# A 32 KB input moved from ScalarE's DMA queue to third place in GpSimd's list of transfers

## The chip, the cores and the metric

One core of a Trainium2 chip. The metric is device microseconds per execution. The state of a run is "fast" unless it lies over 1.5% above the fastest run of its kernel; ratios and comparisons use fast runs alone. A kernel is called faster or slower from 2% on.

In the profiles PE is TensorE, PEld its loads of weights, DVE VectorE, ACT ScalarE, POOL GpSimd and SP SyncE; a name such as ACTq is the part of an engine that issues instructions. q0 is GpSimd's DMA queue, q1 SyncE's and q10 ScalarE's. A packet is a piece of a transfer as the profile lists it; the 4-byte ones at the end of each transfer are called semaphore packets, since the count that a waiting engine looks at (a semaphore) comes with them. A page cuts the span into 40 slices, and a digit is the busy share of a slice in tenths (9 is 90% or more). PEclk is the share of TensorE's full clock that was granted.

## The reference

```python
x: (32, 256) float32, y: (32, 256) float32, weight: (128, 256, 256) float32
out = np.einsum('bi,bj,kij->bk', x, y, weight)        # (32, 128)
```

The weights are 33.55 MB and each is used once for each of the 32 rows of the batch; x and y are 32 KB each.

## The kernel before

The weights come in 32 groups. Two groups (FIRST) are loaded as float32 by SyncE (`w_f`) and cast by ScalarE; thirty are loaded and cast to bfloat16 on the way by GpSimd, in eleven transfers. These grow from 2 MB read to 8 MB and then become ever smaller, so that little work is left after the last. TensorE multiplies them by a block form of x into PSUM, the memory for its sums, used here as eight banks, and VectorE multiplies the sums by y and reduces over j. So y is not needed before the first unit of 16 groups is through TensorE.

```python
sw = [nc.gpsimd.dma_start(out=w_of(groups)[...], in_=rows_of(groups)[...]).then_inc(s, 16).ins
      for (groups, lo, hi), s in zip(LOADS, s_w)]           # eleven transfers
hw = [
    nc.scalar.dma_start(out=x_sb, in_=x).then_inc(s_x, 16).ins,
    nc.scalar.dma_start(out=y_sb, in_=y).then_inc(s_y, 16).ins,
]
for n, g in enumerate(FIRST):
    hw.append(nc.sync.dma_start(out=w_f[:, n:n + 1, :], in_=rows_of((g,))).then_inc(s_f[n], 16).ins)
# ... all of them are put ahead of the barrier that opens the program ...

# VectorE: first x (x_rep, xt, mask, xblk), then y:
t = done(v.transpose(out=yt, in_=y_sb...)._wait_ge(s_y, 16))
t = done(v.tensor_copy(out=y_rep, in_=yt...)._wait_ge(s_dve, t))
# ... four transposes y_rep -> y4 ...

for u, unit in enumerate(UNITS):          # 16, 8, 4, 2, 1, 1 groups
    # ... TensorE waits until the banks are free and each load has landed; matmuls ...
    # VectorE: prod = sums * y4 (frees the banks), acc = reduce(prod)
```

## Time and profile before

| | before |
|---|---|
| time, median of the first 3 runs | 85.0 us (84.89 to 85.02) |
| span of the profiled run | 83.4 us |
| first DMA packet / last weights landed | 1.2 us / 81.06 us |
| PE, DVE, ACT, POOL busy | 32.6, 24.8, 5.3, 8.2 us |
| y: issued / prepared / first used | 0.57 / 13.80 / 57.78 us |

### The profile page before, as it was taken

The page shows a single profiled execution, that of the slowest core. Times are in us where ns is not written, and L with a number is a line of the kernel's source. Part 1 is how long each engine was busy: PE and PEld are TensorE (multiplying, and loading weights), DVE is VectorE, ACT ScalarE, POOL GpSimd, SP SyncE. Part 2 cuts the span into 40 slices and gives each one's busy share as a digit, 9 for nine tenths or more (in the row PEclk, how much of TensorE's full clock was granted, in tenths as well). Part 3 has the DMA queues.
Part 4 walks back from the last instruction along what each step waited for, and adds up shares of the span by engine and source line. Part 5 has one row for each costly group of instructions (what it writes and reads, how often), then busy time and mean ns, then how long its engine had stood idle before and what let it go on. Part 6 is the DMA issues. An engine that isn't in the chain of part 4 may idle for free.

```text
span 83.4 us, 257 instructions
## 1 busy us (share of the span) xinstructions
PE 32.6 (39%) x136; PEld 4.3 (5%) x43; DVE 24.8 (30%) x28; ACT 5.3 (6%) x5; POOL 8.2 (10%) x17
## 2 busy tenths in 40 slices
PE   0000000000000000000099999997009999995780
PEld 0000000000000000000000000000000100112330
DVE  0038595000000000000000000002999900899932
ACT  0039830000000000000000000000000000000000
POOL 5999300000000000000000000000000000000000
PEclk9999999999999999999999999999995699999999
DMA  3999999999999999999999999999999999999980
GB/s 126 383 360 311 216 216 214 210 214 218 214 218 210 214 212 218 218 216 212 212 212 218 216 218 210 214 212 218 216 214 210 218 212 216 218 214 208 203 120 8
DMA packets 4928, 17.91 MB, mean 215 GB/s; under 512 B 384, under 2 KB 832, under 8 KB 4672
## 3 DMA queue, kind: packets, MB, share of 16 engines
q0 software_dynamic: 4400, 15.73, 94.3%
q1 hardware_dynamic: 432, 2.11, 6.7%
q10 hardware_dynamic: 96, 0.07, 0.3%
HBM read 33.62 MB, written 0.02 MB: 404 GB/s over the span
## 4 chain that ended last, share of the span: by engine, by line
DMA 47%; PE 39%; DVE 6%; another core or an unknown queue 2%; POOL 2%; issue 2%; POOLq 0%
DMA w_sb<-in_weight_dram 47%; PE ps L236 39%; DVE tmp L293 5%; POOL w_sb L120 2%; DVE tmp L301 1%; POOL const-float32-0.0 L331 0%; POOLq L331 0%; POOL const-uint8-127 L331 0%; POOL const-float32-1.0 L331 0%; DVE acc L301 0%
## 5 line engine op out<-in xcount | busy, mean ns | idle before, releaser
L236 PE MATMUL ps<-w_sb,xblk 128*128 128x512 bf16 (+1 forms) x136 | 32.6, 398 | 48.7 <-DMA w_sb<-in_weight_dram 43.9
L293 DVE TENSOR_TENSOR tmp<-ps,y 128x4096 f32<-128x4096 f32 (+3 forms) x4 | 8.6, 2153 | 48.4 <-PE ps L236 48.4
L297 DVE TENSOR_REDUCE acc<-tmp 128x16 f32<-128x4096 f32 (+3 forms) x4 | 8.6, 2155 | 0.1
L236 PEld LDWEIGHTS ps<-w_sb,xblk 128*128 128x128 bf16 x43 | 4.3, 101 | 76.9 <-DMA w_sb<-in_weight_dram 42.7
L120 POOL DMA_DIRECT2D w_sb<-in_weight_dram x11 | 7.5, 700 | 0.6 <-issue 0.6
L177 ACT CAST w_sb<-w_f 128x1024 bf16<-128x1024 f32 x4 | 4.0, 1042 | 0.4 <-DMA w_f<-in_weight_dram 0.4
L191 DVE COPY x_rep<-x_sb 32x1024 f32<-32x1024 f32 x1 | 0.7, 724 | 5.6 <-PEq L331 5.6
L226 DVE STREAM_TRANSPOSE y<-y_rep 32x256 f32<-32x256 f32 x4 | 1.7, 435 | 0.1
L197 DVE STREAM_TRANSPOSE xt<-x_rep 32x256 f32<-32x256 f32 x4 | 1.7, 434 | 0.1
L177 ACT ACT_TABLE_LOAD x1 | 1.3, 1283 | 5.5 <-PEq L331 5.5
L209 DVE TENSOR_SCALAR xblk<-xt,mask 128x256 bf16<-128x256 f32 x4 | 1.4, 501 | 0.0
L301 DVE CUSTOM_DVE_ANT_0 tmp<-ps,y 128x256 f32<-128x256 f32 x2 | 0.9, 426 | 1.6 <-PE ps L236 1.4
L221 DVE COPY y_rep<-yt 32x1024 f32<-32x1024 f32 x1 | 0.7, 682 | 0.0
L204 DVE TENSOR_REDUCE mask<-ident 128x4 f32<-128x128 f32 x1 | 0.4, 380 | 1.0 <-POOL ident L168 1.0
L218 DVE STREAM_TRANSPOSE yt<-y_sb 32x256 f32<-32x256 f32 x1 | 0.4, 446 | 0.0
L168 POOL TENSOR_SCALAR_AFFINE_SELECT ident<-ident 128x128 f32<-128x128 f32 x1 | 0.3, 287 | 0.1
L167 POOL MEMSET ident<- 128x128 f32 x1 | 0.3, 289 | 0.0
L301 DVE DVE_READ_ACCUMULATOR2_ANT acc<- 128x1 f32 x2 | 0.2, 84 | 0.0
L331 POOL MEMSET const-float32-0.0<- 128x1 f32 x1 | 0.1, 99 | 0.2 <-issue 0.2
L331 POOL MEMSET const-bfloat16-1.0<- 128x1 bf16 x1 | 0.1, 102 | 0.0
L331 POOL MEMSET const-uint8-127<- 128x1 uint8 x1 | 0.1, 102 | 0.0
L331 POOL MEMSET const-float32-1.0<- 128x1 f32 x1 | 0.1, 99 | 0.0
## 6 DMA issues: line engine op xcount, KB each, us to landing
w_sb<-in_weight_dram POOLq DMA_DIRECT2D x2, 4096.0 KB, 48.5
w_sb<-in_weight_dram POOLq DMA_DIRECT2D x2, 2048.0 KB, 43.6
w_f<-in_weight_dram SPq DMA_DIRECT2D x2, 1024.0 KB, 6.9
w_sb<-in_weight_dram POOLq DMA_DIRECT2D x2, 1024.0 KB, 41.2
w_sb<-in_weight_dram POOLq DMA_DIRECT2D x1, 512.0 KB, 72.6
w_sb<-in_weight_dram POOLq DMA_DIRECT2D x1, 256.0 KB, 73.3
w_sb<-in_weight_dram POOLq DMA_DIRECT2D x1, 128.0 KB, 73.4
w_sb<-in_weight_dram POOLq DMA_DIRECT2D x2, 64.0 KB, 73.1
```

Source lines behind the costliest of these rows:

```text
L120: nc.gpsimd.dma_start(out=w_of(groups)[:, :, lo * J:hi * J], in_=rows_of(groups)[:, :, lo * J:hi * J],).then_inc(s, 16).ins
L177: c = act.copy(out=w_sb[:, place_of[g], lo:hi], in_=w_f[:, n, lo:hi])
L191: t = done(v.tensor_copy(out=x_rep, in_=x_sb.rearrange("b (ip ic) -> b ic ip", ic=IC).unsqueeze(3) .to_broadcast([B, IC, IP, KK]),)._wait_ ...
L197: c = v.transpose(out=xt[q * 32:(q + 1) * 32, :, :], in_=x_rep[:, :, q * IP // Q:(q + 1) * IP // Q, :],)
L204: t = done(v.tensor_reduce(out=mask, in_=ident.rearrange("p (ip kk) -> p kk ip", kk=KK), axis=AX, op=add,)._wait_ge(s_pool, 2))
L209: c = v.tensor_scalar(out=xblk[:, :, :, kk], in0=xt, scalar1=mask[:, kk:kk + 1], scalar2=None, op0=mult,)
L221: t = done(v.tensor_copy(out=y_rep, in_=yt.unsqueeze(3).to_broadcast([B, J // 32, B, KK]),)._wait_ge(s_dve, t))
L226: c = v.transpose(out=y4[q * 32:(q + 1) * 32, :].rearrange("p (jb j) -> p jb j", j=32), in_=y_rep[:, :, q * BQ:(q + 1) * BQ, :],)
L236: return pe.add_instruction(mybir.InstMatmult(name=nc.get_next_instruction_name(), engine=mybir.EngineType.PE, ins=[pe.lower_ap(rhs), pe.l ...
L293: t = done(v.tensor_tensor(out=prod, in0=sums, in1=y4.unsqueeze(1).to_broadcast([P, n_g, J]), op=mult,)._wait_ge(s_pe, n_pe))
L297: done(v.tensor_reduce(out=acc[:, unit[0]:unit[-1] + 1:unit[1] - unit[0]], in_=prod, axis=AX, op=add,)._wait_ge(s_dve, t))
L301: done(v.tensor_tensor_reduce(out=prod[:, 0, :], in0=sums[:, 0, :], in1=y4, scale=1.0, scalar=0.0, op0=mult, op1=add, accum_out=acc[:, uni ...
```

## The change

The intent is to clear the beginning: y no longer stands in a hardware queue beside `w_f`, and ScalarE has one issue less. y is loaded where there is time for it, behind the first two weight transfers.

```diff
+    sw.insert(2, nc.gpsimd.dma_start(out=y_sb, in_=y).then_inc(s_y, 16).ins)
+
     hw = [
         nc.scalar.dma_start(out=x_sb, in_=x).then_inc(s_x, 16).ins,
-        nc.scalar.dma_start(out=y_sb, in_=y).then_inc(s_y, 16).ins,
     ]
```

Nothing else moves on any engine.

## The prediction

> **What bounds the kernel now.** I read the slices of the span first, to see which resource never rests; then the chain that ended last, in order of time, to see where the end is set; then the DMA issues and the timeline of the first microseconds, because the change sits there.
>
> The slices and queues on the page:
>
> ```profile
> span 83.4 us, 257 instructions
> ...
> DMA  3999999999999999999999999999999999999980
> ...
> q0 software_dynamic: 4400, 15.73, 94.3%
> q1 hardware_dynamic: 432, 2.11, 6.7%
> q10 hardware_dynamic: 96, 0.07, 0.3%
> HBM read 33.62 MB, written 0.02 MB: 404 GB/s over the span
> ```
>
> The 16 DMA engines are full in 37 of 40 slices, from about 2 us to about 80 us, while PE works 39% of the span and DVE 30%. Nearly all of it is q0, the weights that GpSimd issues. The file of weights is 33.55 MB (128 x 256 x 256 x 4 bytes), so the time is the time to read it, plus a start and a tail.
>
> The chain of waits, in order of time (start, length, what):
>
> ```profile
> 2.65 39.16 DMA w_sb<-in_weight_dram
> ...
> 41.86 15.90 PE ps L236 x64
> ...
> 57.78 4.44 DVE tmp L293
> ...
> 62.32 8.75 PE ps L236 x32
> 71.07 0.08 another core or an unknown queue
> ...
> 74.81 1.19 another core or an unknown queue
> ...
> 77.93 0.53 another core or an unknown queue
> ...
> 79.53 0.18 another core or an unknown queue
> ...
> 81.10 0.30 PE ps L236
> ...
> 81.42 0.43 DVE tmp L301
> ```
>
> The page counts 47% for DMA and 39% for PE, but the reader should not take PE for a second bound. Each matmul group from 71 us on waits again for a transfer (the steps called "unknown queue"; the timeline names the releaser of 76.04, 78.50 and 79.75 as DMA of the weights). PE, which starts at 41.86 only when the third load has landed, has caught up with the stream by 71.07 and then follows it. What comes after the last landing is short: one matmul of 0.30 us, one DVE pass of 0.43 us and the output transfer. So the end is the instant when the last weight byte lands, near 81.06 us, plus a fixed tail of 2.3 us. A delay in PE's start is forgiven up to 0.08 + 1.19 + 0.53 + 0.18 = about 2.0 us before it moves the end; a delay of the stream is forgiven nowhere.
>
> The first microseconds and the two transfers of the change:
>
> ```profile
> 0.12 0.41 ACTq L128 DMA_DIRECT2D x_sb<-in_x_dram  x1
> ...
> 0.57 0.44 ACTq L129 DMA_DIRECT2D y_sb<-in_y_dram  x1
> 1.06 7.53 POOL L120 DMA_DIRECT2D w_sb<-in_weight_dram  x11 [0.61 <-issue]
> 5.55 1.28 ACT L177 ACT_TABLE_LOAD   x1 [5.55 <-PEq L331]
> 5.59 0.72 DVE L191 COPY x_rep<-x_sb 32x1024 f32<-32x1024 f32 x1 [5.59 <-PEq L331]
> ...
> 10.78 0.45 DVE L218 STREAM_TRANSPOSE yt<-y_sb 32x256 f32<-32x256 f32 x1
> 11.26 0.68 DVE L221 COPY y_rep<-yt 32x1024 f32<-32x1024 f32 x1
> 11.97 1.83 DVE L226 STREAM_TRANSPOSE y<-y_rep 32x256 f32<-32x256 f32 x4
> ```
>
> y is issued at 0.57 us, is prepared by DVE from 10.78 to 13.80 us without any wait, and is first used by the product at 57.78 us: 44 us of slack. The page of issues gives its way to landing:
>
> ```profile
> x_sb<-in_x_dram ACTq DMA_DIRECT2D x1, 32.0 KB, 1.7
> y_sb<-in_y_dram ACTq DMA_DIRECT2D x1, 32.0 KB, 4.5
> ```
>
> x and y are equally large, but y needs 4.5 us: its packets wait behind the first megabyte of w_f on the same engines. That wait also costs nothing today.
>
> **What the Trainium skill says.** "DMA: Bandwidth & Descriptors", section "Issuing engines are not separate DMA queues": transfers run on the same 16 DMA engines whichever engine issues them, and issuing from several saves only sequencer time. The trace agrees as far as it can: between 5.7 and 8.4 us q0 and q1 each have about half of the engines and the total stays where it was. So moving y should move its work, not remove it. Same page, "Queues, rings and completion order": each DMA engine takes turns between queue rows packet by packet. In this trace the turn is coarse: y, issued at 0.57, is served between 3.6 and 4.7 us, after most of the first w_f. Same page, "Why a DMA increments its semaphore by 16 and not by 1": a transfer from GpSimd posts on all 16 engines, and 32 rows split evenly over 16. The trace shows that shape for y already: 32 packets of 1 KB and 16 of 4 bytes. Same page, "Specifications", has a first byte after about 1 us for GpSimd's path and 0.6 us for ScalarE's; with tens of microseconds of slack the 0.4 us does not matter, and in this trace q0's first packet comes at 5.6 us, with w_f ahead of it.
>
> **The change part by part.**
>
> Removed from ScalarE: one issue of 0.44 us. ScalarE then sits until 5.55 us in the opening barrier, released by others. Worth on the path: 0.
>
> Removed from the early stream: y's packets. Between 3 and 5 us they took 1.69 us of engine time in all (32 packets of about 46 ns, 16 of 9 ns), over 16 engines 0.106 us. The engines were full from 1.4 us on, so w_f and everything behind it come about 0.1 us earlier.
>
> Added to GpSimd: one issue, third of 12. The eleven have a mean of 700 ns, the small ones 548 to 616 ns, so I take 0.57 us. The nine later loads are issued that much later, the last at 8.57 in place of 8.00 us. The first two loads (6 MB read) keep q0 occupied until about 22 us (their landings are at 12.6 and 22.3 us); the third load's issue slips from 2.65 to about 3.2 us, so q0 has 19 us of work in hand. Worth: 0.
>
> The opening barrier: GpSimd joins it at 5.35 us, when its sixth issue of eleven has begun; its sequencer runs about five issues ahead. With twelve, it would join about when the seventh begins, at 5.9 us. DVE's and ScalarE's first work then starts 0.5 to 0.6 us later, and the mask and the copies of w_f end near 12 us in place of 11.2. PE does not start before 41.86. Worth: 0.
>
> Added to the stream q0: 32 packets of 1 KB and 16 semaphore packets, between load two and load three. q0's nearest packets, 512 bytes written from 1 KB read, take 60 ns and its semaphore packets 22 ns; per engine 2 x 60 + 22 = 0.142 us. Packets overlap somewhat at the end of the stream (0.25 us there held 101 packets, 40 ns per packet and engine), so it may be nearer 0.10 us. I take 0.12.
>
> DVE: yt now waits for y, which lands just after load two, near 22.4 us. A new idle of about 11 us appears before that transpose, and y's work of 3.0 us ends near 25.5 us in place of 13.8. The first product at 57.78 is still 32 us away. Worth: 0.
>
> Sum for the last landing: -0.106 + 0.12 = about +0.01 us, anywhere from -0.03 to +0.05. PE's start moves by the same amount. The tail is unchanged. Predicted time: 85.0 us, as before.
>
> **The rivals.**
>
> 1. *The small transfer breaks the stream.* If q0 had to drain at y's end, each engine would idle for the time of a round trip; x alone in an empty machine needs 1.7 us from issue to landing, so this could cost up to about 1.5 us (86.5 us, just within 2%). Against it: q0 already passes ten ends of transfers, and around the landing of load two, at 21.9 to 22.3 us, the engines stay as full as before. Even the last four loads, of 32 to 256 packets, follow one another without a hole. Chance about 3%.
>
> 2. *The early part gets faster.* If y's packets hold up w_f and thereby q0's start by more than their own time, removing them would win some tenths: 84.5 to 84.8 us. For it: q0's first packet comes only at 5.6 us, 4.5 us after its issue. Against it: in the meantime q1 keeps all engines busy, so an earlier q0 only changes the order of the same bytes.
>
> 3. *GpSimd becomes the bound at the start.* If 0.57 us more of issuing, or a longer descriptor ring (275 packets an engine in q0 now, 278 after), delayed q0's first packet, DMA would go idle. w_f alone would last until about 6.9 us (2.1 MB at the 380 to 390 GB/s of 2 to 6 us), so q0 may slip by 1.3 us unnoticed; and y stands third, so the first two issues do not move at all. If the ring were full at 276, GpSimd would pause and the late loads would still come many microseconds ahead of need. Time: 85.0 to 85.2 us.
>
> 4. *y arrives too late.* If it were served after all weights it would set the end. The place in the list forbids it: 22 us against a need at 57.8 us.
>
> **Range and chances.** The sum is under 0.1 us, the three runs of before span 0.13 us, and rivals 2 and 3 reach 0.3 to 0.5 us at most. I give 85.0 us, with 84.7 to 85.3 us to hold eight times in ten. The borders of 2% are 83.3 and 86.7 us. No part of the change can give 1.7 us, since the stream keeps its bytes; only an unforeseen break of the stream could cost it. Faster 1%, within 2% 97%, slower 2%.
>
> **What would show it right or wrong.** Right: the DMA row full from the second slice to the 38th; q10 halved to 48 packets and q0 at 4448; the sum of the queues' shares unchanged; DVE's yt waiting for y until about 22.4 us and working until about 25.5; GpSimd's twelve issues near 8.1 us; DVE's first copy near 6.1 us; PE starting within 0.1 us of 41.86; the last landing within 0.1 us of 81.06. Wrong: a slice near 22 us under full (rival 1), a start of PE earlier than 41.6 us (rival 2), a dip in the third or fourth slice (rival 3), or a first product later than 57.8 us by more than PE's own shift (rival 4).

## More of the kernel before

One view is missing there: who waited for whom, longest first (engine, line, what it waited for: us in total, times, longest).

```profile
DVE tmp L293 <- PE ps L236: 48.4, 2, 44.0
PE ps L236 <- DMA w_sb<-in_weight_dram: 43.9, 4, 41.9
...
PE ps L236 <- DVE tmp L293: 4.6, 1, 4.6
```

No line has y in it: nobody waited for it. The large waits are for weights. The last line will matter: TensorE's second unit waits 4.6 us for VectorE's first product, since the first unit fills all eight banks. That is how a late y could do harm.

## The result, and the profile after

| | before | after |
|---|---|---|
| median of 6 runs each | 84.94 us (84.89 to 85.02) | 84.92 us (84.73 to 84.94) |
| ratio, 95% interval | | 0.9991 (0.9978 to 1.0004) |
| last weights landed (one trace each) | 81.06 us | 81.13 us |

A ratio is the mean time of one kernel's fast runs over that of the other's fast runs of the same rounds, so it is not quite the ratio of the medians. It is the same time. The page of the changed kernel, its slices and queues:

```profile
DMA  4999999999999999999999999999999999999980
...
q0 software_dynamic: 4432, 15.76, 94.3%
q1 hardware_dynamic: 432, 2.11, 6.8%
q10 hardware_dynamic: 48, 0.03, 0.1%
```

The DMA row is as full as before, also in the eleventh slice (20.9 to 22.9 us), where y now passes. ScalarE's queue q10 has lost half of its packets; GpSimd's q0 has gained 32.

The chain of the changed kernel (start, length, what):

```profile
2.65 0.52 POOL y_sb L127
3.17 38.71 DMA w_sb<-in_weight_dram
...
41.93 15.77 PE ps L237 x64
...
74.83 1.28 another core or an unknown queue
...
81.17 0.30 PE ps L237
```

y's issue has entered the chain with 0.52 us, and the step behind it has become shorter by 0.45 us: 38.71 in place of 39.16. That is a trap in reading a chain. The third weight transfer was issued later, but it was issued 19 us before its turn, so the wait behind the issue took up the delay and TensorE began at 41.93 in place of 41.86 us.

The timeline, for the parts that moved:

```profile
2.64 0.53 POOL L127 DMA_DIRECT2D y_sb<-in_y_dram  x1
...
6.08 0.79 DVE L192 COPY x_rep<-x_sb 32x1024 f32<-32x1024 f32 x1 [6.08 <-PEq L332]
...
22.48 0.43 DVE L219 STREAM_TRANSPOSE yt<-y_sb 32x256 f32<-32x256 f32 x1 [10.95 <-DMA y_sb<-in_y_dram]
...
23.67 1.83 DVE L227 STREAM_TRANSPOSE y<-y_rep 32x256 f32<-32x256 f32 x4
```

The opening barrier ends 0.5 us later, as GpSimd has one more issue to get through, and VectorE waits 10.95 us for y. Both are new, both are large beside the effect on the time, and neither costs anything. The first product is 32 us away.

### The profile page after: what moved, and what is told of

It is laid out like the page before. It is cut to its first block, busy times and chain, and to the rows that moved or that the text cites. A ratio compares the mean times of both kernels' runs of the same rounds, so it can differ in the third digit from the quotient of the medians.

```text
span 83.4 us, 257 instructions
## 1 busy us (share of the span) xinstructions
PE 32.6 (39%) x136; PEld 4.3 (5%) x43; DVE 25.1 (30%) x28; ACT 5.2 (6%) x5; POOL 8.8 (11%) x18
## 3 DMA queue, kind: packets, MB, share of 16 engines
q0 software_dynamic: 4432, 15.76, 94.3%
## 4 chain that ended last, share of the span: by engine, by line
DMA 46%; PE 39%; DVE 6%; POOL 3%; another core or an unknown queue 3%; issue 2%; POOLq 0%
DMA w_sb<-in_weight_dram 46%; PE ps L237 39%; DVE tmp L294 5%; POOL w_sb L120 2%; POOL y_sb L127 1%; DVE tmp L302 1%; POOL const-float32-0.0 L332 0%; POOLq L332 0%; POOL const-uint8-127 L332 0%; POOL const-float32-1.0 L332 0%; DVE acc L302 0%
## 5 line engine op out<-in xcount | busy, mean ns | idle before, releaser
L127 POOL DMA_DIRECT2D y_sb<-in_y_dram x1 | 0.5, 534 | 0.0
```

What stands on the lines that cost most here:

```text
L127: sw.insert(2, nc.gpsimd.dma_start(out=y_sb, in_=y).then_inc(s_y, 16).ins)
```

## The experiments

The theory under test: the time is set by the stream of transfers, y costs that stream its own packets wherever it stands, and everything else (issue, barrier, y's landing) lies in slack. The rivals: a small transfer breaks the stream; the crowded beginning was the cost; GpSimd's issuing sets the start; the third place matters.

### What one small load costs the stream, on either queue

A change of 0.1 us or less cannot be seen in 85 us, so the load was multiplied. Eight more copies of y go into spare tiles, behind the original, once on each queue. VectorE waits for all.

```diff
+    for n in range(8):    # nine_pool: in the changed kernel
+        sw.insert(3 + n, nc.gpsimd.dma_start(out=y_more[n], in_=y).then_inc(s_ym[n], 16).ins)
```

> The changed kernel with eight more copies of y loaded by GpSimd right behind y (into spare tiles, VectorE waits for all before it prepares y). Theory (the stream of transfers sets the end and a small transfer costs only its own packets, 96 + 22 ns per engine as measured for y): 8 x 0.118 us = 0.94 us more, or 0.89 if packets overlap as the weights' do; time 85.8 us. Rival (each end of a transfer drains the queue, 1 to 1.5 us each): 93 to 97 us. Rival (small transfers hide beside the big ones): 84.9 us.

```diff
+    for n in range(8):    # nine_act: in the kernel before
+        hw.append(nc.scalar.dma_start(out=y_more[n], in_=y).then_inc(s_ym[n], 16).ins)
```

> The kernel before with eight more copies of y loaded by ScalarE right behind y. Theory (same work on the same engines, whoever issues): 8 x 0.106 us = 0.85 us more than before, time 85.8 us, within 0.15 us of the nine loads by GpSimd. Rival (the place matters: at the beginning there is spare room, in the stream there is none): 84.9 to 85.2 us here against 85.8 there.

| | median | ratio to before (95%) |
|---|---|---|
| nine loads by GpSimd | 85.6 us | 1.0086 (1.0071 to 1.0100) |
| nine loads by ScalarE | 85.96 us | 1.0126 (1.0107 to 1.0145) |
| before, same rounds | 84.88 us | |

Both are slower by about what packets cost, and by nothing like the 8 to 12 us of a drained queue. Eight loads more by ScalarE make 0.0126 x 84.88 = 1.07 us, 0.134 us each. Eight more by GpSimd, against a kernel of the same rounds that has one (y_first, below, 0.9992), make 0.0094 x 84.88 = 0.80 us, 0.10 us each (both to about 0.02 us, from the intervals). The expectation that the two runs would lie within 0.15 us of each other failed: they are 0.34 us apart (0.0040 x 84.88), the intervals do not overlap, and the small loads on ScalarE's queue cost more. The queue line of each page says where (queue, kind: packets, MB, share of 16 engines); first the nine loads by ScalarE, then those by GpSimd:

```profile
q10 hardware_dynamic: 480, 0.33, 1.5%
```

```profile
q0 software_dynamic: 4688, 16.02, 94.4%
```

q10 grew from 96 to 480 packets, 48 a load, and from 0.3% to 1.5% of the engines. From the single packets, which the trace keeps behind these rounded shares, the time in q10 went from 0.231 to 1.268 us per engine, 0.130 us a load; in q0 from 78.648 in the changed kernel to 79.523, 0.109 us a load. GpSimd's loads have 32 packets each (4688 - 4432 = 8 x 32). So the packets account for both costs, and a load by GpSimd is cheaper by 0.02 to 0.03 us. On ScalarE's queue the 1 KB packets took 56 ns and the 4-byte ones 17 ns on average, where those of y alone took about 46 and 9 ns. The two runs differ in the queue and in the place (the crowded beginning, the middle of the stream); which of them lengthens the packets was not tested.

### No y at all

```diff
-    sw.insert(2, nc.gpsimd.dma_start(out=y_sb, in_=y).then_inc(s_y, 16).ins)
+    t = done(v.memset(y_sb, 1.0))        # VectorE, ahead of the transpose; the result is wrong on purpose
```

> No load of y at all (y is set to one by VectorE, so the result is wrong on purpose). Theory: the stream is shorter by y's own packets alone, 0.1 us: 84.8 us. That bounds what any other place of y can win. Rival (y's queue or its issue disturbs the start, whoever issues it): 84.0 to 84.5 us.

Measured: 84.69 us, ratio 0.9974 (0.9958 to 0.9991), and a wrong result. So 0.22 us less, with an interval from 0.08 to 0.36 us. The 0.1 us expected is within it, and the 0.4 us at the near edge of the rival's range is just outside. The saving shows in the times alone: in the one trace of each, the last weights landed at 81.09 us without y and at 81.06 before. This is the most that any place of y can win: about a quarter of a per cent.

### y in other places of the list

Each is the changed kernel with another number in `sw.insert`: 0 (first), 3 (fourth), 4 (fifth).

> y as the first of GpSimd's list in place of the third. Theory: the first weights are issued 0.53 us later, but the engines are busy with w_f until then, so 84.9 us, first weight packet between 5.6 and 6.2 us, no hole in the DMA row. Rival (GpSimd's issue sets the start of the stream): 85.4 to 85.5 us.

Measured: 84.79 us, 0.9992 (0.9976 to 1.0008). The first weight is issued 0.68 us later (1.74 in place of 1.06 us), and the first weight packet of q0 comes at 6.2 us in place of 5.6; the packets that q0 has from 5.5 us on are y's. The DMA row still shows 9 in every slice from the second to the 38th, for the engines are busy with `w_f` meanwhile. So what the rival feared does not happen.

> y as fourth in GpSimd's list, behind the third load. It lands near 42 us and is prepared by about 45 us, still 12 us ahead of the first product. Theory (only the deadline of the first product counts): 84.9 us. Rival (the third place is special): more than 85.3 us.

Measured: 84.83 us, 0.9998 (0.9977 to 1.0019). VectorE waits 30.6 us for y and begins with it at 42.1 us; it costs nothing.

> y as fifth, behind the fourth load. It lands near 61.5 us, is prepared at 64.6 us, 6.8 us after the first product could have begun. Theory (PE waits for the bank that this product frees; part of the delay is forgiven): following VectorE's and PE's queue of work from there gives 88.5 to 90.3 us. Rival (the end follows the last weight alone): 85 us.

Measured: 89.97 us, 1.0608 (1.0556 to 1.066), inside the expected range. The chain:

```profile
61.38 0.44 DVE yt L219
...
64.51 4.44 DVE tmp L294
...
69.05 9.39 PE ps L237 x32
...
78.46 2.30 DVE tmp L294
```

y is there only at 61.38 us, the first product begins at 64.51 in place of 57.72 us, and TensorE has the banks for its second unit at 69.05 in place of 62.26 us. So the third place is nothing special: first, third and fourth are one time, and the border lies between the fourth place and the fifth, where y's preparation ends 12 us before and 6.7 us after the first product could begin.

### How much lateness of the first product is forgiven

y_fifth delayed the product by 6.8 us and cost 5 us. To measure alone how much of such a delay is forgiven, an additional product of k groups is put ahead of the first one on VectorE, into a spare tile.

```diff
+        if u == 0:
+            done(v.tensor_tensor(out=spare[:, :k, :], in0=sums[:, :k, :],
+                in1=y4.unsqueeze(1).to_broadcast([P, k, J]), op=mult)._wait_ge(s_pe, n_pe))
         if n_g > 1:
             t = done(v.tensor_tensor(out=prod, in0=sums, ...
```

k = 4:

> The additional product with 4 groups (128x1024, 1.21 us). VectorE's queue after its second product forgives 1.7 us, by the trace of the kernel before; so 84.9 us where PE runs at full clock, up to 85.4 us in runs in which the second group of matmuls falls into the half clock as with 7 groups. If nothing were forgiven: 86.1 us.

k = 7:

> The changed kernel with an additional product of 7 groups (128x1792, about 2.0 us) on VectorE ahead of the first product, so that the banks are freed and PE resumes 2.0 us later. The prediction forgave 2.0 us, counted from PE's waits for transfers: then 84.9 us. If VectorE's own queue is tighter (its products at 75.6, 78.0 and 79.6 us follow one another within 0.1 us, and only 1.4 us are free ahead of the last one): 0.5 us more, 85.4 us.

k = 16:

> The same with all 16 groups, about 4.45 us of delay. Forgiven 2.0 us: 87.3 us. Forgiven 1.4 to 1.5 us: 87.9 us. Nothing forgiven: 89.3 us. All forgiven: 84.9 us.

| k | added | median | ratio to before (95%) |
|---|---|---|---|
| 4 | 1.2 us | 85.1 us | 1.0028 (1.0000 to 1.0056) |
| 7 | 2.0 us | 86.01 us | 1.0115 (1.0074 to 1.0156) |
| 16 | 4.4 us | 87.62 us | 1.0298 (1.0256 to 1.0340) |

With k = 7, forgiveness of 2.0 us would have left the time as it was; it rose by 0.0115 x 84.9 = 0.98 us, more than either case expected (84.9 or 85.4 us). One of the six runs with k = 7, at 86.62 us, counts as slow; it is in the median and not in the ratio. The chain for k = 7 shows what became the bound:

```profile
64.61 9.91 PE ps L238 x32
...
74.54 2.30 DVE tmp L300
...
76.87 2.29 DVE acc L304
79.16 1.14 DVE tmp L300
...
83.20 0.34 DVE tmp L308
```

From 74.54 us on it is VectorE without a pause, to 83.54 us: 9.00 us of its own work. In the kernel before, the same work begins at 71.11 us and could end at 80.11, and it ends at 81.86 because it waits for the last weights; so VectorE's queue forgives 1.75 us. In this trace it began 3.43 us late: 2.02 us for the added product, and most of the rest from TensorE, whose 32 matmuls took 9.91 in place of 8.75 us and whose first unit ended 0.35 us later. 3.43 - 1.75 = 1.68 us, which is the delay of the end (83.54 against 81.86). The clock row of the page explains the slower matmuls; before, then k = 7:

```profile
PEclk9999999999999999999999999999995699999999
```

```profile
PEclk9999999999999999999999999999655559999997
```

The spell of half clock lasts about five slices in place of two. How long it lasts differs from run to run (mean granted clock 0.934 to 0.960 in these fast runs), and their times are spread over 1.2 us, while the kernel before is spread over 0.4 us. k = 16 went the other way. Its chain and clock row:

```profile
66.39 8.37 PE ps L238 x32
...
74.78 2.30 DVE tmp L300
```

```profile
PEclk9999999999999999999999999999955589999999
```

Here the second unit begins when most of the spell is over, and takes 8.37 us. By the clock records of the three traces, 3.41 us of this unit ran at half clock before, 5.76 us with k = 7 and 2.64 us with k = 16; less half of that, its 32 matmuls took 7.04, 7.03 and 7.05 us. So the clock accounts for the whole difference. Over the runs with k = 16 the time rose by 0.0298 x 84.9 = 2.53 us of 4.42 added: 1.9 us were forgiven (1.5 to 2.25 by the interval), against 1.0 us with k = 7 (0.7 to 1.4).

So what is forgiven is not one number. VectorE's queue allows 1.75 us after the second unit (1.88 us, reckoned in the same way from the trace of the changed kernel), and TensorE's second unit adds to it or takes from it, as more or less of it falls into the spell of half clock. A longer spell alone cost nothing: it lasts 6.8 us in the traces without y and with x moved (below), and these runs are no longer than the others. With k = 4, where 84.9 to 85.4 us was expected, the six runs fall into two sets, three at 84.77 to 84.94 and three at 85.26 to 85.39 us; the mean clock does not separate them, and this stays open.

### x as well, and the changed kernel once more

```diff
-        nc.scalar.dma_start(out=x_sb, in_=x).then_inc(s_x, 16).ins,
+    sw.insert(1, nc.gpsimd.dma_start(out=x_sb, in_=x).then_inc(s_x, 16).ins)
```

> x goes to GpSimd's list as well, behind the first weights, so that ScalarE issues nothing. x lands near 12.6 us, and PE's other operand is ready near 17 us, 25 us before PE begins. Theory A (x's packets now run before w_f's first packet, in engines that are otherwise idle, so they are free where they are): 0.1 us slower than the changed kernel, 85.0 us. Theory B (x stands ahead of w_f in the engines and delays it): 0.1 to 0.2 us faster, first w_f packet before 1.3 us in place of 1.4.

Measured: 84.93 us, 1.0003 (0.9983 to 1.0023). The first packet of `w_f` still comes at 1.4 us with nothing ahead of it, so theory B's mechanism is absent. Theory A's cost of 0.1 us is too small to be told from none here: the single traces have the last weights at 81.26 in place of 81.13 us, which agrees with it but is one trace each.

> The changed kernel, unaltered, once more. The runs with nine loads differ by 0.0040 in their ratios, which over nine loads makes 0.04 us per load in favour of GpSimd; so 0.9991 to 1.0000, not to be told from the same. If the change wins more than its own packets: under 0.998.

Measured: 84.92 us, 1.0001 (0.9980 to 1.0023), as expected. No version was found that beats both kernels.

## Why the prediction was right

The time was predicted as 85.0 us and is 84.92. By its steps:

- **The bound.** Right. Eight more small loads in either place lengthen the run by about the time of their packets, while a barrier 0.5 us later, a wait of 11 or even 30 us on VectorE and an issue 0.5 us later leave it as it is.
- **The issue by GpSimd.** Taken as 0.57 us, measured 0.53; the barrier moved DVE's first copy to 6.08 us (predicted near 6.1). Placing y first instead shows that even 0.68 us ahead of all weights costs nothing.
- **ScalarE's copies.** The prediction had the mask and the copies of `w_f` end near 12 us in place of 11.2. The copies still end at 11.2: they used to wait 0.41 us for the second load into `w_f`, and that wait took up the delay. VectorE's preparation of x ended at 11.5 us. A size was off, in slack.
- **The packets added.** Predicted 32 packets of 1 KB and 16 of 4 bytes, q0 at 4448. It is 4432: y went as 16 packets of 2 KB, 96 ns each, and 16 of 4 bytes, 9 ns each. (The 22 ns that the prediction took for a semaphore packet, and that the expectation of the nine loads called measured for y, are those of the weight loads.) So y cost 96 + 9 = 105 ns per engine, against a sum of 142 ns that the prediction lowered to 0.12 us for overlap. Its parts were wrong and only the total came near, which was partly luck; the nine loads put it at 0.10 to 0.11 us.
- **The packets removed.** Taken as 0.106 us. The trace before gives that for y alone; the nine loads give 0.13 us for each load in a crowd. So the balance is about 0 by the packets of the one load, and -0.02 to -0.03 us if a load in a crowd stands for it, which is not shown. Predicted was +0.01, from -0.03 to +0.05. The direct comparison can't tell these apart (0.9978 to 1.0004 is 0.19 us less to 0.03 us more).
- **y's new time.** Predicted to land near 22.4 and be ready near 25.5 us; measured 22.46 and 25.5.
- **What is forgiven.** The one step that failed as put: "about 2.0 us", from adding TensorE's waits along the chain. Once the product is late, the chain runs through VectorE's queue, which allows 1.75 us, and the half clock moves the sum: 1.0 us was forgiven with k = 7, 1.9 us with k = 16, which alone would not speak against 2.0. The change never drew on this reserve (TensorE's start moved by 0.07 us), so the result did not depend on it; a change that delays the product by 2 us would have been predicted about 1 us too fast.

Rival 1 fell to the nine loads. Rival 2 fell to the comparison itself: it needs 0.2 to 0.5 us, and the change saved 0.19 us at most. (The run without y, 0.22 us less, lies in its range and does not speak against it.) Rival 3, whose own figures reach 0.2 us and not the 0.3 us that the range gives it, fell to y in first place, and 4 was fenced in between the fourth and the fifth place.

## What to carry to other kernels

When one resource is busy from end to end, a small transfer costs its own packets and its queue hardly matters; choose its place by its deadline, which is a date that the trace gives, and leave some transfers between. To size an effect below the noise, multiply it until it shows, and have it in both places. When adding up what is forgiven, follow every engine's queue to the end, not only the waits along the chain that ended last.

## What the Trainium skill lacked or had wrong

- "DMA: Bandwidth & Descriptors", section "Issuing engines are not separate DMA queues": it has the choice of issuing engine save sequencer time alone. Nearly so here, not wholly: nine loads of 32 KB took 0.34 us longer (0.0040 of 84.88 us) on ScalarE's queue at the beginning than on GpSimd's in the stream, with 0.130 against 0.109 us of engine time for each additional load. Queue and place differ together, so which of them costs it is not shown.
- The same page, section "Anatomy of one DMA — SWDGE (gpsimd) path": its fit has a fixed part of about 2.0 us for each transfer, which it puts down mostly to completion. For a load in a full stream that part is not paid by the stream: eight more loads added 0.10 us each. A line for this case would help.
- The same page, section "Queues, rings and completion order": an engine drains a packet of about 9 to 17 descriptors from one queue before it turns to the next. In the trace before, y's first packet came at 3.6 us, 3.0 us after its issue, when 96 of `w_f`'s packets of 8 KB had begun, six for each engine; from then on those of y and of `w_f` took turns nearly one by one. If the profile's packets are the page's descriptors, that is a finer turn than it says. Whether the engine was bound to the six, or y's packets were not ready earlier, is not shown.
- The same page tells over how many engines a load is split, but no page was found that says how an engine's two rows of y become packets: 32 packets of 1 KB and 16 of 4 bytes from ScalarE, 16 of 2 KB and 16 of 4 bytes from GpSimd.
